# The norm's root in the up and gate stages: spread over the partitions by a store and a broadcast load instead of a matmul with a diagonal

## The chip, the cores and the metric

The kernel runs on one core of a Trainium2 chip. The metric is the device time of one execution in microseconds, the median of several runs. A core has TensorE (PE, matmuls; its weight loads are shown as PEld), VectorE (DVE), ScalarE (ACT), GpSimd (POOL) and SyncE (SP). SP, ACT and POOL also issue the transfers between the core's memory and DRAM, each in the order of its own queue: an issue that has to wait holds up what stands behind it on that engine.

## The reference

One layer of a streaming encoder on 512 tokens with 2048 channels, in float32. Cut to what matters here:

```
h = rms_norm(x, norm_mix_w);  proj = h @ w_in            # attention and gated linear attention, 16 units here
x = x + concat(y_attention, y_linear) @ w_out            # stage "wo"
h = rms_norm(x, norm_ffn_w)
u = causal_depthwise_conv(h @ w_ffn_up)                  # stage "up", 44 units
x = x + (gelu(u_gate) * u_val) @ w_ffn_down              # stages "dn0", "dn1", "dn2"
h = rms_norm(x, norm_ple_w)
g = sigmoid(h @ w_ple_gate)                              # stage "pg", 8 units
x = x + g * (p @ w_ple_proj)
return rms_norm(x, final_norm_w)
```

`rms_norm(x, w)` is `x * rsqrt(mean(x*x) + 1e-6) * w`, with one root per token. The root is a factor of a whole token, so it can be multiplied in after the matmul. This is what the kernel does in "up" and "pg": the channels' weights go into the operand, the matmul runs on the un-normalised values, and its result is multiplied by the root.

## The kernel before

Channels lie on the 128 partitions and tokens along the free dimension: a tile of activations is 128 x 512, and a unit of a stage makes two such tiles. Each stage's matrix product is cut by a Strassen-like scheme into seven products (P1, P2, P6, P5, P7, P3, P4 in `PLAIN`, L33) of blocks and sums of blocks. Each operand is held as a rounded part and a remainder, and a product is made of three passes over its blocks: 24 matmuls of 128x128 by 128x256 with 8 blocks.

**Steps.** The host code writes the order of the work out as a list of steps, one product of one unit each. The first two units of a stage are interleaved product by product (14 steps), and so are the last two. A step `i` does, in this order: the items of an agenda that are due now (`k` 0 and 1), the rounded half of the weight page of step `i + 2` on ScalarE (`prep_high`), its remainder on VectorE (`prep_low`), its own 24 matmuls, then later agenda items, the norm's step, and the read-out of the product from PSUM into the unit's tile `u` (`collect`; the first product of a quarter on ScalarE, the others on VectorE). Weight pages are named `l` (loaded as they are) or `s` (sums of blocks), and the two halves go to one of three places in the tile `w` in turn, so the page of step `i + 2` can be made once product `i - 1` is done. The engines work through their instructions in the order in which they were written; they run ahead of each other as far as the waits on data and buffers allow. The loads of weight pages are issued on SP whenever a page becomes free (`issue`, L430), with POOL adding a second block to some of them. Scratch copies for later stages (`dn_S`, `pg_S`) use the same queues.

**The norm.** In the stages marked `chained` (and `wo` excepted) the sum of squares `acc` (128 x 512) of the stage before is complete only while the first pair of units runs. `norm_step` (L1106) is called after the matmuls of each step with the step's number within the stage:
- at 11, `mean_square` (L1081) makes four matmuls against a column of ones: the mean square of each token, now with tokens on the partitions (128 x 4, in `ms`);
- after the read-out of step 11, `norm_root` (L1121) adds epsilon on VectorE and takes the square root on ScalarE;
- at 12, `rstd_end` (L1095) takes the reciprocal and does one Newton step on VectorE: four small instructions on `tok`. The root then has to come from 128 x 4 to a tile `rb` that has all 512 tokens on each of the 128 partitions. VectorE multiplies the identity by each of the four columns (`dg`, four blocks of 128 x 128, a diagonal each);
- at 13, TensorE multiplies a matrix of ones with `dg` in float32, 128 x 512, into the PSUM bank `pb`, in which each row is now the whole root;
- at 14, ScalarE copies `pb` to `rb`.

**Who reads `rb`.** In "up" each unit's tile is multiplied by `rb` at the start of `after_up` (L680), in "pg" at the start of `after_gate` (L719; the sigmoid follows a step later in ScalarE's order). When a unit's items begin is set by `pace` and `late` (L1618 to L1624): the first unit of "up" not before step 22 of the stage, the first unit of "pg" not before step 15. `late` shifts a unit by some steps more; its key counts the unit from the end of the stage.

Of the kernel before, what the change touches and what calls it, by code (L numbers as in the profile page):

```python
# [8 lines left out]
F32 = mybir.dt.float32  # L9
F32R = mybir.dt.float32r  # L10
I32 = mybir.dt.int32
AF = mybir.ActivationFunctionType
ALU = mybir.AluOpType

P = 128
T = 512
# [4 lines left out]
TT = T // P  # L21
# [21 lines left out]
def encoder_block(ctx: ExitStack, tc: tile.TileContext, A, out):  # L43
    nc = tc.nc
# [3 lines left out]
    tp = ctx.enter_context(tc.tile_pool(name="tmp", bufs=1))  # L48
# [21 lines left out]
    vec, act, ten = InOrder(nc.vector), InOrder(nc.scalar), InOrder(nc.tensor)  # L70
# [8 lines left out]
    ident = cp.tile([P, P], F32, name="ident")  # L79
    make_identity(nc, ident)  # L80
    ones = cp.tile([P, P], F32, name="ones")
# [8 lines left out]
    rb = cp.tile([P, T], F32, name="rb")  # L90
# [19 lines left out]
    late = []  # L110
# [9 lines left out]
    def psum_aux(name):  # L120
        return aux[0](name)
# [171 lines left out]
    def scratch(name, shape):  # L293
        return dp.tile(list(shape), F32, name=name)
# [214 lines left out]
    def prep(i, own=None):  # L509
        prep_low(prep_high(i, own))  # L510

    def prep_high(i, own=None):
        if i >= len(steps):
            return None
        unit, prod = steps[i]
        name = PRODUCTS[prod][0]
        n = unit.stage.kb * P
        make(unit, name)
        if prod == unit.order[0] and unit.sums in ("dve", "s3"):
            make(unit, "S1")  # L520
        if i + 1 < len(steps):
            nxt, p = steps[i + 1]
            q = PRODUCTS[p][0]
            if (nxt is unit or nxt.paired) and (q != "S4" or "P6" in nxt.w) and (unit, q) != (front.units[6], "S2"):
                make(nxt, q)
        if i > 0 and steps[i - 1][1] == "P6" and steps[i - 1][0].paired:
            make(steps[i - 1][0], "S4")
        key = name
        if unit.sums != "memory":
            key = {"S4": "S2"}.get(name, "L21" if name == "S3" and unit.sums != "dma" else name)  # L530
        raw = unit.w[key]
        hi, lo = own or weight_pages(places.get(i, 24))
        act.activation(hi[:, :n], raw[:, :n], AF.Copy)
        unit.w[prod] = hi, lo
        return unit, key, hi[:, :n], lo[:, :n], raw[:, :n]

    def prep_low(p):
        if p:
            unit, key, hi, lo, raw = p
            vec.tensor_tensor(lo, raw, hi.bitcast(F32), ALU.subtract)  # L540
            used(unit, key)
# [7 lines left out]
    def product(unit, prod, at=None, between=None):  # L549
        if prod == "PP":  # L550
            return embedding(unit)
        _, op, b = PRODUCTS[prod]
        fresh = b not in unit.banks
        if fresh:
            unit.banks[b] = bank("acc" + b)
        t = unit.banks[b][1][:, 0:256]
        hi, lo = unit.w[prod]
        st = unit.stage
        kb = st.kb

        for p in range(3):
            for k in range(kb):
                if p * kb + k == at:
                    between()
                x = st.piece(op, k)[:, p % 2]
                w = (hi, hi, lo)[p][:, k * P:k * P + P]
                kw = {} if fresh else {"skip_group_check": True}
                ten.matmul(t, w, x, start=fresh and p == k == 0, stop=p == 2 and k == kb - 1, **kw)
# [33 lines left out]
    def load_x(src, unit):  # L602
        unit.xs = page("c", "xs").rearrange("p (s t) -> p s t", s=2)
        load = nc.sync.dma_start(unit.xs, src[unit.u])
        if unit.stage is wo and unit.pos < 3:
            tc.keep_in_program_order(load)
# [56 lines left out]
    def after_norm(dst, xd, col):  # L663
        def after(unit):
            if unit.last is not None:
                return [(1, 0, lambda: nc.sync.dma_start(dst[unit.u], unit.xs))] + squares(unit, 6 + unit.last * 2)
            return [(0, 1, lambda: residual(dst, unit)), (1, 2, lambda: weighted(col, unit)),
                    (2, 1, lambda: store_pair(xd, unit.u, unit.o[:, 0, :], unit.o[:, 1, :]))] + squares(unit, 3 + (unit.head == 1))
        return after
# [49 lines left out]
    def after_gate(unit):  # L719
# [9 lines left out]
    stages = [Stage("wo", list(range(8)), 8, mixd, blk2(A["w_out"]), after_norm(streams[1], h2d, nffn), "s3", "dma", ends=("memory", None),  # L729
                    begin=lambda u: load_x(streams[0], u), begin_at=10, chained=True)]  # L730
# [176 lines left out]
    for ci, n in enumerate(CHUNKS):  # L907
# [2 lines left out]
                            "dve", "dma", begin=(lambda u: load_x(streams[1], u)) if ci == 2 else None, begin_at=0, late={},  # L910
                            ends=("memory" if ci != 1 else None, "memory" if ci == 2 else None)))
    stages.append(Stage("pg", list(range(8)), 8, h3d, blk2(A["w_ple_gate"]), after_gate, "dma", "dma", last=HALVES, ends=("memory", None),
                        begin=load_gate, begin_at=9, chained=True, pace=(15, 5.3), late={}))
    summed = [u for st in (stages[0], stages[1], stages[2], stages[5], stages[4]) for u in st.units if u.sums == "memory"]
    assert [u.stage.name for u in summed[::2]] == ["wo", "up", "dn0", "pg", "dn2", "dn2"]
    stages[4].quarter = last_quarter(lambda: stages[7], nple)
# [6 lines left out]
    base = {}  # L923
# [26 lines left out]
    for a, b in zip(stages[2:], stages[3:]):  # L950
        i0 = base[a.units[-1]]
        for n, p in enumerate(PLAIN):
            op = PRODUCTS[p][1]
            for g in range(2):
                start = 2 * n + 2 + g
                if g and b.chained:
                    start = max(start, 5)
# [123 lines left out]
    def mean_square(c):  # L1081
        n = (c.stop - c.start) // P
        ms = psum_aux("ms")
        for t in range(n):
            ten.matmul(ms[:, t:t + 1], acc[:, c.start + t * P:c.start + t * P + P], ones[:, 0:1], start=True, stop=True)
        return ms[:, :n]
# [8 lines left out]
    def rstd_end(w):  # L1095
        n = w.shape[1] // 4
        a, y, t, r = (w[:, n * q:n * q + n] for q in range(4))
        vec.reciprocal(y, y)
        vec.tensor_tensor(t, y, y, ALU.mult)
        vec.scalar_tensor_tensor(t, t, -0.5, a, ALU.mult, ALU.mult)  # L1100
        vec.scalar_tensor_tensor(r, t, 1.5, y, ALU.add, ALU.mult)
        return r

    norm = {}

    def norm_step(i):  # L1106

        if i == 11:
            norm["ms"] = mean_square(slice(0, T))
        elif i == 12:  # L1110
            norm["dg"] = tp.tile([P, T], F32, tag="dg", name="dg")
            r = rstd_end(norm["w"])
            for t in range(TT):
                vec.tensor_scalar(norm["dg"][:, t * P:(t + 1) * P], ident, r[:, t:t + 1], None, ALU.mult)
        elif i == 13:
            norm["pb"] = psum_aux("pb")
            ten.matmul(norm["pb"], ones, norm["dg"], start=True, stop=True)
        elif i == 14:
            act.activation(rb, norm["pb"], AF.Copy)

    def norm_root():  # L1121
        norm["w"] = rstd_begin(norm["ms"])
# [456 lines left out]
    for i, (unit, prod) in enumerate(steps[:-4]):  # L1579
        st = unit.stage  # L1580
        now[0] = i
        todo = sorted(agenda[i], key=lambda x: x[0])
        for k, f in todo:
            if k == 0:
                f()

        behind = i == base[front.units[6]]
        if not behind:
            coming = prep_high(i + 2) if i < len(steps) - 5 else None
        for k, f in todo:  # L1590
            if k == 1:
                f()
        if behind:
            coming = prep_high(i + 2)
        prep_low(coming)
        product(unit, prod)
        for k, f in todo:
            if 1 < k < 9:
                f()
        if st.chained and st is not wo:  # L1600
            norm_step(i - base[st.units[0]])
        if i == len(steps) - 5:
            add_gated(units[-2], 1, lo_half)
        if i - len(steps) in EARLY:
            p, op, g = EARLY[i - len(steps)]
            t = xtile(op, g, "last")
            prep(len(steps) + p, (t[:, 0, :], t[:, 1, :]))
        collect(unit, prod)
        for k, f in todo:
            if k == 9:  # L1610
                f()
        if st.chained and st is not wo and unit.head is not None and i == base[unit] + 11:
            norm_root()
        if st is stages[-1] and unit.last is not None:
            if prod == "P4" and unit is units[-2]:
                times_norm(unit, 1, lo_half)
        elif prod == unit.order[-1]:
            begin = i + 1  # L1618
            if st.pace:
                begin = max(begin, base[st.units[0]] + int(st.pace[0] + st.pace[1] * unit.pos))  # L1620
            if unit.pos - len(st.units) in st.late:
                begin += st.late[unit.pos - len(st.units)]
            for at, k, f in st.after(unit):
                agenda[begin + at].append((k, f))  # L1624
# [211 lines left out]
```

## Time and profile before

| | |
|---|---|
| Runs before | 2201.5 us median of 3 (2201.16 to 2205.98) |
| Span of the profiled execution | 6266.3 us; no other time of that execution is recorded |
| TensorE busy, instructions | 6253.6 us, 18248 |
| VectorE busy | 1910.0 us |
| ScalarE busy | 1349.7 us |
| GpSimd busy | 215.6 us |
| Granted TensorE clock | 1.000 |
| Moved by DMA | 561.39 MB, 200037 packets |
| Up stage's `ms` matmuls, spreading matmul | start at 2614.51 and 2631.21 us |
| Gate stage's `ms` matmuls, spreading matmul | start at 5920.51 and 5937.21 us |

The page shows one execution taken by the hardware profiler. Its span is 2.85 times the median of the timed runs, so a place in the trace is not a place in time of a timed run. A row of the order of time reads: start, duration, engine, line, operation, written tile<-read tiles, engine shape (TensorE only), shapes, count, and in brackets the idle time of the engine before it and what ended it. Rows of TensorE stand for several matmuls in a row (x24 is one product). SPq and ACTq are the issues of transfers on these engines; the list of DMA issues gives, at the end of a row, the median time from issue to landing. Nearly all work has line 64, the helper that records instructions, so tiles tell the places apart.

### The profile page before, as it was taken

To read this page: it belongs to the slowest core of one execution; us is meant where nothing else is said; L and a number is where in the kernel's file an instruction comes from. 1 tells how busy PE (TensorE), PEld (TensorE's weight loads), DVE (VectorE), ACT (ScalarE), POOL (GpSimd) and SP (SyncE) were. 2 spreads that over 40 slices of the span, in tenths; PEclk is the share of its full clock that TensorE was granted. 3 is DMA by queue.
4 is the path that set the end of the run, shared out by engine and by line. 5 is a ranking of instruction groups with operands and counts; after the bars stand their busy time and mean duration, and the time that the engine had idled before them with its cause. 6 is when DMAs were issued, how large, how long until landed. Compare 5 with 4: busy or idle time off the path is not lost.

```text
span 6266.3 us, 45637 instructions
## 1 busy us (share of the span) xinstructions
PE 6253.6 (100%) x18248; PEld 5819.7 (93%) x18248; DVE 1910.0 (30%) x2585; ACT 1349.7 (22%) x1960; POOL 215.6 (3%) x261
## 2 busy tenths in 40 slices
PE   9999999999999999999999999999999999999999
PEld 5555999988989799999999999999999999999999
DVE  2222222222222233333333333333333232233333
ACT  2111111222221222222222222222222121222322
POOL 0000000000000000000000000000000000000000
DMA  1123222222222334344444443333333242333432
GB/s 67 34 81 64 61 71 57 72 74 63 70 70 87 110 100 122 101 108 116 113 113 103 112 107 92 83 78 87 79 108 95 61 113 70 109 101 114 121 110 88
DMA packets 200037, 561.39 MB, mean 90 GB/s; under 512 B 21808, under 2 KB 64048, under 8 KB 199824
## 3 DMA queue, kind: packets, MB, share of 16 engines
q1 hardware_dynamic: 163184, 431.28, 21.0%
q0 software_dynamic: 34656, 124.27, 11.5%
q8 instruction: 143, 2.34, 0.2%
q10 hardware_dynamic: 1984, 2.92, 0.1%
q14 instruction: 70, 0.57, 0.0%
HBM read 484.99 MB, written 119.54 MB: 96 GB/s over the span
## 4 chain that ended last, share of the span: by engine, by line
PE 100%; DVE 0%; issue 0%; DVEq 0%; ACT 0%; POOL 0%; POOLq 0%
PE accA L64 48%; PE accC L64 24%; PE accB L64 12%; PE v L64 5%; PE vaA L64 2%; PE vaC L64 1%; PE pp L64 1%; PE psc L64 1%; PE ptr L64 1%; PE py L64 1%; PE po L64 1%; PE vaD L64 1%; PE vaB L64 1%; PE plr L64 0%; PE pu L64 0%; PE pat L64 0%
## 5 line engine op out<-in xcount | busy, mean ns | idle before, releaser
L64 PE MATMUL accA<-h,w 128*128 128x256 f32 x5088 | 1695.5, 563 | 0.0
L64 PEld LDWEIGHTS accA<-h,w 128*128 128x128 f32 x5088 | 1673.7, 473 | 13.1 <-issue 11.6
L64 PE MATMUL accC<-h,w 128*128 128x256 f32 x4248 | 1347.7, 542 | 0.0
L64 PEld LDWEIGHTS accC<-h,w 128*128 128x128 f32 x4248 | 1330.8, 454 | 1.6 <-issue 0.6
L64 DVE TENSOR_TENSOR w<-s,w 128x1024 fp32r<-128x1024 f32 (+1 forms) x381 | 458.4, 1203 | 1100.4 <-ACT w L64 1100.4
L64 DVE TENSOR_TENSOR w<-l,w 128x1024 fp32r<-128x1024 f32 (+1 forms) x320 | 383.2, 1197 | 612.1 <-ACT w L64 607.6
L64 ACT ACTIVATE u<-accA 128x256 f32<-128x256 f32 x302 | 116.1, 384 | 2033.4 <-PE accA L64 2033.4
L64 ACT ACTIVATE w<-l 128x1024 fp32r<-128x1024 f32 (+1 forms) x320 | 331.8, 1037 | 956.1 <-PE accC L64 557.4
L64 ACT ACTIVATE w<-s 128x1024 fp32r<-128x1024 f32 (+1 forms) x381 | 395.0, 1037 | 327.5 <-PE accB L64 203.2
L64 PE MATMUL accA<-up_R,w 128*128 128x256 f32 x1056 | 325.3, 531 | 0.0
L64 PE MATMUL accA<-up_N,w 128*128 128x256 f32 x1056 | 324.2, 530 | 0.0
L64 PE MATMUL accB<-up_R,w 128*128 128x256 f32 x1056 | 323.7, 529 | 0.0
L64 PEld LDWEIGHTS accA<-up_R,w 128*128 128x128 f32 x1056 | 320.5, 441 | 1.6 <-issue 0.8
L64 PEld LDWEIGHTS accA<-up_N,w 128*128 128x128 f32 x1056 | 320.6, 442 | 0.0
L64 PEld LDWEIGHTS accB<-up_R,w 128*128 128x128 f32 x1056 | 320.5, 442 | 0.0
L64 PE MATMUL v<-w,h 128*128 128x512 f32 x384 | 318.6, 1100 | 0.0
L64 PEld LDWEIGHTS v<-w,h 128*128 128x128 f32 x384 | 165.2, 431 | 150.5 <-issue 150.1
L64 DVE TENSOR_TENSOR s<-s,l 128x1024 f32<-128x1024 f32 (+1 forms) x176 | 211.2, 1200 | 0.0
L64 DVE TENSOR_TENSOR u<-u,accC 128x256 f32<-128x256 f32 x102 | 43.0, 421 | 547.7 <-PE accC L64 547.7
L64 DVE TENSOR_TENSOR u<-u,accA 128x256 f32<-128x256 f32 x98 | 41.3, 421 | 510.4 <-PE accA L64 510.4
L64 DVE TENSOR_TENSOR u<-u,accB 128x256 f32<-128x256 f32 x100 | 42.1, 421 | 479.4 <-PE accB L64 479.4
L64 ACT ACTIVATE u<-accC 128x256 f32<-128x256 f32 x98 | 37.7, 384 | 603.5 <-PE accC L64 603.5
(303 smaller groups left out, 5554.9 us busy)
## 6 DMA issues: line engine op xcount, KB each, us to landing
l<-in_w_up SPq DMA_DIRECT2D x132, 512.0 KB, 3.5
s<-in_w_up SPq DMA_DIRECT2D x84, 512.0 KB, 3.5
s<-in_w_up POOLq DMA_DIRECT2D x84, 512.0 KB, 5.5
l<-in_w_dn SPq DMA_DIRECT2D x56, 448.0 KB, 3.4
l<-in_w_blk SPq DMA_DIRECT2D x48, 512.0 KB, 3.5
s<-in_w_blk SPq DMA_DIRECT2D x32, 512.0 KB, 3.5
s<-in_w_blk POOLq DMA_DIRECT2D x32, 512.0 KB, 6.1
l<-in_w_out SPq DMA_DIRECT2D x28, 512.0 KB, 3.6
```

The lines of the kernel that those rows point to most:

```text
L64: ins = f(*args, **kw)
```

## The change

The diagonal, the spreading matmul and the copy out of PSUM are gone. In their place, at step 12, the root (128 x 4, in core memory) is stored to a scratch tensor `rootd` of 4 x 128 words in DRAM, transposed on the way, so that the 512 tokens lie in a row. Later `rb` is loaded from it with the same row read for all 128 partitions. In "up" both transfers are issued on SP, the load at step 14. In "pg" both are issued on ScalarE's queue, the load at step 13, and the first unit's items after its products begin one step later than before (`late={-8: 1}`: the eighth unit from the end is the first).

```diff
     stages.append(Stage("pg", list(range(8)), 8, h3d, blk2(A["w_ple_gate"]), after_gate, "dma", "dma", last=HALVES, ends=("memory", None),
-                        begin=load_gate, begin_at=9, chained=True, pace=(15, 5.3), late={}))
+                        begin=load_gate, begin_at=9, chained=True, pace=(15, 5.3), late={-8: 1}))
...
     norm = {}
+    rootd = scratch("rootd", (TT, P))
 
-    def norm_step(i):
+    def norm_step(i, load, queue):
 
         if i == 11:
             norm["ms"] = mean_square(slice(0, T))
         elif i == 12:
-            norm["dg"] = tp.tile([P, T], F32, tag="dg", name="dg")
-            r = rstd_end(norm["w"])
-            for t in range(TT):
-                vec.tensor_scalar(norm["dg"][:, t * P:(t + 1) * P], ident, r[:, t:t + 1], None, ALU.mult)
-        elif i == 13:
-            norm["pb"] = psum_aux("pb")
-            ten.matmul(norm["pb"], ones, norm["dg"], start=True, stop=True)
-        elif i == 14:
-            act.activation(rb, norm["pb"], AF.Copy)
+            queue.dma_start(rootd.rearrange("t p -> p t"), rstd_end(norm["w"]))
+        elif i == load:
+            queue.dma_start(rb, rootd.rearrange("t p -> (t p)")[None, :].broadcast_to([P, T]))
...
         if st.chained and st is not wo:
-            norm_step(i - base[st.units[0]])
+            norm_step(i - base[st.units[0]], *((13, nc.scalar) if st is stages[-1] else (14, nc.sync)))
```

How this moves the instructions on the queues that wait or are waited for is shown in the prediction, where it is used: on ScalarE in the first pair of "pg", and on SP in the first pair of "up". On TensorE nothing moves but for the row `pb<-dg,ones`, which is gone in both stages:

```order
L64 MATMUL accA<-h_102,w 128x256 x7
L64 MATMUL pb<-dg,ones 128x512
L64 MATMUL accA<-pg_R_23315,w 128x256
```

This is the order before, at the end of step 13 of "pg"; in the change the first matmul of step 14 follows the last one of step 13.

## The prediction

> **What bounds the kernel now.** I read the page first (engines, then the chain that ended last), then the order of time around the two stretches the change touches.
>
> ```profile
> span 6266.3 us, 45637 instructions
> PE 6253.6 (100%) x18248; PEld 5819.7 (93%) x18248; DVE 1910.0 (30%) x2585; ACT 1349.7 (22%) x1960; POOL 215.6 (3%) x261
> PE 100%; DVE 0%; issue 0%; DVEq 0%; ACT 0%; POOL 0%; POOLq 0%
> ```
>
> TensorE bounds the profiled execution from end to end. But that execution spans 6266.3 us and the timed median is 2201.5 us, 0.351 of it, and nothing in the page explains the difference. So a sum made in the trace does not carry over as it stands. Two readings are possible. In the *even* reading every duration shrinks by 0.351. In the *PE-only* reading the profiled execution merely ran TensorE's instructions slowly, and VectorE, ScalarE and DMA keep their durations. The second passes the test it could fail: VectorE's 1910.0 us fit into 2201.5 us (87%). It is the stricter one for this change, because waits that 7 us products hide in the trace may show under shorter ones. I work with PE-only and keep the even reading as a bound.
>
> The unit of time is one product of 24 matmuls, one step of the agenda. Two neighbours of the gate stage start 7.17 us apart:
>
> ```profile
> 5968.14 7.34 PE L64 MATMUL accA<-h,w 128*128 128x256 f32 x24
> 5975.31 7.34 PE L64 MATMUL accC<-h,w 128*128 128x256 f32 x24
> ```
>
> 7.17 x 0.351 = 2.52 us is my estimate for a timed product.
>
> **What the matmul with the diagonal costs.** The up stage first: the two last products of the first pair (one row of 48 matmuls), the spreading matmul, and the next unit's products.
>
> ```profile
> 2616.77 14.60 PE L64 MATMUL accA<-h,w 128*128 128x256 f32 x48
> 2620.27 0.88 DVE L64 TENSOR_SCALAR dg<-ident,tok 128x128 f32<-128x128 f32 x4
> 2631.21 2.64 PE L64 MATMUL pb<-dg,ones 128*128 128x512 f32 x2
> 2632.48 8.55 PE L64 MATMUL accA<-up_R,w 128*128 128x256 f32 x24
> 2633.56 7.01 PEld L64 LDWEIGHTS accA<-up_R,w 128*128 128x128 f32 x23 [0.83 <-issue]
> 2633.89 0.60 ACT L64 ACTIVATE rb<-pb 128x512 f32<-128x512 f32 x1 [1.15 <-PE pb L64]
> 2640.74 7.34 PE L64 MATMUL accB<-up_R,w 128*128 128x256 f32 x24
> ```
>
> From 2616.77 to 2640.74 are 23.97 us for three products of 7.17 (21.51) and pb: pb makes 2.46 us of difference. 1.27 of it is pb's own place (2631.21 to 2632.48), the rest is the next product starting slowly behind it (the 0.83 us before its second weight load). The gate stage is the same:
>
> ```profile
> 5922.64 14.74 PE L64 MATMUL accA<-h,w 128*128 128x256 f32 x48
> 5923.12 1.04 ACT L64 ACTIVATE w<-l 128x1024 fp32r<-128x1024 f32 x1
> 5924.20 1.23 DVE L64 TENSOR_TENSOR w<-l,w 128x1024 fp32r<-128x1024 f32 x1 [1.22 <-ACT w L64]
> 5925.74 0.36 DVE L64 SCALAR_TENSOR_TENSOR tok<-tok 128x4 f32<-128x4 f32 x2
> 5926.14 0.87 DVE L64 TENSOR_SCALAR dg<-ident,tok 128x128 f32<-128x128 f32 x4
> 5930.37 0.39 ACT L64 ACTIVATE u<-accA 128x256 f32<-128x256 f32 x1 [6.20 <-PE accA L64]
> 5930.65 1.05 ACT L64 ACTIVATE w<-l 128x1024 fp32r<-128x1024 f32 x1
> 5937.21 2.64 PE L64 MATMUL pb<-dg,ones 128*128 128x512 f32 x2
> 5937.41 0.38 ACT L64 ACTIVATE u<-accA 128x256 f32<-128x256 f32 x1 [5.71 <-PE accA L64]
> 5938.48 8.42 PE L64 MATMUL accA<-pg_R,w 128*128 128x256 f32 x24
> 5938.77 1.23 DVE L64 TENSOR_TENSOR w<-s,w 128x1024 fp32r<-128x1024 f32 x1 [5.82 <-ACT w L64]
> 5940.52 1.23 DVE L64 TENSOR_TENSOR u<-u,rb 128x1024 f32<-128x1024 f32 x1 [0.53 <-ACT rb L64]
> 5946.74 7.34 PE L64 MATMUL accB<-pg_R,w 128*128 128x256 f32 x24
> ```
>
> 24.10 - 21.51 = 2.59 us. Both together: 5.05 us at most; by the even reading 5.05 x 0.351 = 1.77 us at least, as long as TensorE is the bound there. I take pb's own place unshrunk and let the slow start behind it go, 2 x 1.27 = **2.5 us gained**: a pass over 512 columns is real work, while the gap before a weight load belongs to the slow issue of this execution.
>
> The four diagonal tiles on VectorE (0.88 and 0.87 us) and the copy to rb on ScalarE (0.60 us, twice) go too. I cost them at nothing: ScalarE sits idle for 5.71 and 6.20 us and VectorE for 5.82 us before the next product's work in these rows, and in the PE-only reading VectorE still has 13% free. Were VectorE the bound in both stretches, its 1.75 us would be the gain instead, less than the 2.5.
>
> **What the store and the load cost.** No transfer of 4-byte pieces occurs before, so the store (512 of them, 128 partitions x 4) is bounded by other rows.
>
> ```profile
> q1 hardware_dynamic: 163184, 431.28, 21.0%
> g_N<-tp SPq DMA_DIRECT2D x44, 128.0 KB, 1.8
> bias<-in_bias SPq DMA_DIRECT2D x16, 256.0 KB, 2.5
> wo_S<-in_w_out SPq DMA_DIRECT2D x8, 512.0 KB, 4.6
> dn_S<-dn_S POOLq DMA_DIRECT2D x8, 448.0 KB, 8.2
> ```
>
> Below: 1.8 us, the fastest landing. Above: q1's packets average 0.21 x 16 x 6266.3 / 163184 = 0.129 us; 512 over 16 engines are 32 x 0.129 = 4.1 us, on top of 1.8 makes 5.9. The slowest row, 8.2 us, is the far end. I take 4 us. The load writes 256 KB, as bias does: 2.5 us (1.8 to 4.6).
>
> The Trainium skill, DMA: Bandwidth & Descriptors, section Rules for kernel authors, speaks against such a store: a strided last dimension becomes one descriptor per element. In its section Anatomy of one DMA a transfer (of GpSimd's kind) has a fixed part of about 2.0 us, and its section Bandwidth has 10.5 ns for a small packet: as an estimate from this page the store would take 2.0 + 32 x 0.0105 = 2.3 us, nothing would wait for it, and the sum would be 2199.0. No trace so far has such a store.
>
> Gate stage, ScalarE's order, before and in the change (l and s are weight pages whose rounded half goes to w, accA is read out of PSUM into u):
>
> ```order
> L64 ACTIVATE tok<-tok 128x4
> L64 ACTIVATE w<-l_23819 128x1024
> L64 ACTIVATE u<-accA 128x256
> L64 ACTIVATE w<-l_23851 128x1024
> L64 ACTIVATE u<-accA 128x256
> L64 ACTIVATE w<-s_24176 128x1024
> L64 ACTIVATE rb<-pb 128x512
> ```
>
> ```order
> L64 ACTIVATE tok<-tok 128x4
> L64 ACTIVATE w<-l_23814 128x1024
> L1112 DMA rootd<-tok 128x4x1
> L64 ACTIVATE u<-accA 128x256
> L64 ACTIVATE w<-l_23846 128x1024
> L1114 DMA rb<-rootd 128x512
> L64 ACTIVATE u<-accA 128x256
> L64 ACTIVATE w<-s_24167 128x1024
> ```
>
> Two waits have come into ScalarE's queue: for VectorE's root ahead of step 13's read-out and weight page, and for the store's landing ahead of step 14's page, which step 16's product needs. Count from the start of step 12 (5922.64), with timed products of 2.52 us:
> - The root is done at 5926.10 - 5922.64 = 3.5. Nothing in that chain waits for a later product, so it does not shrink. ScalarE issues the store, reads out accA (0.39) and makes the page of step 15 (1.05): done at about 5.4, needed at 3 x 2.52 = 7.6. Hidden by 2.2 us.
> - The store lands at 3.5 + 0.4 + 4 = 7.9 (5.7 to 12.1). Load issue 0.4, read-out 0.38, page 1.05: step 16's page is ready at 9.7 (7.5 to 13.9) and needed at 4 x 2.52 = 10.1. At my value it is hidden by 0.4 us; at the far end TensorE stands still for 3.8 us. The next page, step 17's, follows one read-out and page later: 11.2 against 12.6.
> - rb arrives at 8.3 + 2.5 = 10.8. VectorE's first use was moved one step, behind the low halves of steps 16 and 17 and the read-out of step 15 (which ends at 10.1) and a sum of 1.2 us, so not before 11.7. Hidden.
>
> I book 0.5 us of loss here for a store somewhat slower than 4 us. If the cover were gone, the cost would be the 3.8 us above.
>
> Up stage, SP's order in the change:
>
> ```order
> L64 DMA s_9067<-in_w_up 128x1024
> L1112 DMA rootd<-tok 128x4x1
> L458 DMA dn_S_9164<-in_w_dn 128x1024
> L64 DMA s_9198<-in_w_up 128x1024
> L1114 DMA rb<-rootd 128x512
> L64 DMA l_9228<-in_w_up 128x1024
> L64 DMA l_9232<-in_w_up 128x1024
> ```
>
> Before, the same weight and dn_S loads stand there without the two L111x rows. What queues behind the load's wait are the l pages of the unit after next.
>
> ```profile
> 2622.34 0.33 SPq L64 DMA_DIRECT2D s<-in_w_up  x1
> 2641.07 0.38 ACT L64 ACTIVATE u<-accA 128x256 f32<-128x256 f32 x1 [6.58 <-PE accA L64]
> 2642.43 1.23 DVE L64 TENSOR_TENSOR w<-s,w 128x1024 fp32r<-128x1024 f32 x1 [8.43 <-ACT w L64]
> 2643.69 7.48 SPq L64 DMA_DIRECT2D l<-in_w_up  x3
> ```
>
> The s page went out only after the root anyway (2622.34 against 2620.27). The three l pages go out behind VectorE's half of the page that ScalarE makes after reading out step 14, in my count at 3 x 2.52 + 0.4 + 1.05 + 1.2 = 10.2; SP is free again between 5.7 and 12.1, so they are up to 2 us late, with more than one unit (7 x 2.52 = 17.6 us) before they are read. Nothing. rb is first read at step 22 in this stage, some 20 us after the root. Nothing. POOL's queue is not touched: 244 rows before and after.
>
> **The sum.** -2.5 + 0.5 = -2.0 us. Against the profiled execution's span, where 7.17 us products hide every wait, it would be 6266.3 - 5.05 = 6261.3; on the timed median 2201.5 - 2.0 = **2199.5 us**.
>
> **Rivals.**
> - *ScalarE's wait decides* (slower). At the far end the store lands at 12.1, and step 16 starts 3.8 us late: -2.5 + 3.8 = +1.3, so 2202.8. It decides once the store needs more than 4.4 us; past about 10.5 us, with the read-outs and pages queued up behind it, the loss passes 6.5 us and the result 2205.9. For it: 512 pieces are something this kernel never sent. Against: 8.2 us is a row of accumulating transfers of 448 KB.
> - *The matmul was not on the path* (no change). If in the timed run TensorE waits for VectorE or ScalarE in the paired products anyway, taking pb out moves the wait: 2201.5. For it: VectorE at 87% on average, and these steps also split the operands. Against: the idle time before VectorE's rows is 5 us of 7.17 here.
> - *The whole stall goes* (faster). If the slow start behind pb is real time too, 5.05 us go and nothing comes: 2196.5. For it: the 0.83 us gap stands behind both pb's. Against: it would have to be the one thing that does not shrink in a run 2.85 times as fast.
> - *Even reading*: 1.77 us go, every wait is hidden as in the trace: 2199.7, the forecast within noise.
>
> **How the numbers follow.** Forecast with the even reading 0.52; not on the path 0.20; whole stall 0.16; ScalarE's wait 0.12. About 0.2% (4.4 us) is what a measurement of this kernel can tell from no change; the three runs before span 4.8 us. Faster than 2197.1: the whole stall and some spread of the forecast, 0.20. Slower than 2205.9: the tail of ScalarE's wait and the spread of the runs, 0.09. The rest, 0.71, is no change. The range takes the whole stall below and ScalarE's wait with the before runs' spread above: 2196.0 to 2205.5.
>
> **What would show it.** Right: no pb row in either stretch, the products around both places 7.17 us apart throughout, the profiled span some 5 us shorter; the store landing within 6 us of its issue; no idle time of VectorE before the first u<-u,rb named after DMA. Wrong: idle time of ScalarE ending with the store, longer than 4.4 us; a weight page landing after its first reader is ready; or a time outside 2196.0 to 2205.5, which means that the shape of the timed run differs from both readings.

## The result and the profile after

The changed kernel takes 2211.86 us (median of 5 runs, 2210.13 to 2214.03), the kernel before 2201.5 us (5 runs, 2199.93 to 2205.98). The ratio is 1.0039, with an interval of 1.0028 to 1.0051: slower by 6 to 11 us, where 2 us of gain were forecast, and outside the range of 2196.0 to 2205.5. Single executions of 3127.87 us (the kernel before, granted clock 0.653) and 5677.53 us (an experiment, 1.000) also occurred and stand in no ratio here; the profiled execution of 6266.3 us on which the prediction rests resembles the second.

So the profile of the changed kernel, which runs at the timed speed, needs a partner that does the same. The kernel before was profiled again (experiment e_before below). Its page, engines of it:

```profile
span 2204.8 us, 45637 instructions
PE 2182.9 (99%) x18248; PEld 2132.2 (97%) x18248; DVE 1874.5 (85%) x2585; ACT 1321.6 (60%) x1960; POOL 215.1 (10%) x261
```

And the page of the changed kernel, span and engines:

```profile
span 2208.4 us, 45624 instructions
PE 2179.6 (99%) x18244; PEld 2130.6 (96%) x18244; DVE 1873.2 (85%) x2577; ACT 1319.7 (60%) x1958; POOL 214.9 (10%) x261
```

The busy times fell, as instructions are gone: TensorE by 3.3 us, VectorE by 1.3, ScalarE by 1.9. The span did not. By busy times alone the change would be a gain; the loss is time in which TensorE, though 99% busy on average, does nothing or works slowly in one place. That place is the gate stage. From the start of its `ms` matmuls to the end of the span, the kernel before takes 2204.8 - 2062.24 = 142.6 us and the changed one 2208.4 - 2056.45 = 151.9 us, 9.4 us more (in the text below: "the tail"; one execution each, and two kernels that are equal from there on differ by 0.7). Its first steps before, in the order of time:

```profile
2062.24 1.02 PE L64 MATMUL ms<-ones,acc 128*128 128x1 f32 x8
2063.13 5.69 PE L64 MATMUL accA<-h,w 128*128 128x256 f32 x48
2069.20 1.13 PE L64 MATMUL pb<-dg,ones 128*128 128x512 f32 x2 [0.38 <-DVE dg L64]
2069.76 3.30 PE L64 MATMUL accA<-pg_R,w 128*128 128x256 f32 x24
...
2072.90 2.89 PE L64 MATMUL accB<-pg_R,w 128*128 128x256 f32 x24
```

The same steps in the changed kernel; ACTq rows are ScalarE's issues of transfers:

```profile
2056.45 1.05 PE L64 MATMUL ms<-ones,acc 128*128 128x1 f32 x8
2057.36 5.90 PE L64 MATMUL accA<-h,w 128*128 128x256 f32 x48
2062.16 0.36 DVE L64 SCALAR_TENSOR_TENSOR tok<-tok 128x4 f32<-128x4 f32 x2
2062.56 0.38 ACTq L1112 DMA_DIRECT2D rootd<-tok  x1
2063.10 2.99 PE L64 MATMUL accA<-pg_R,w 128*128 128x256 f32 x24
2065.92 2.99 PE L64 MATMUL accB<-pg_R,w 128*128 128x256 f32 x24
2074.30 0.33 ACTq L1114 DMA_DIRECT2D rb<-rootd  x1
2074.67 0.38 ACT L64 ACTIVATE u<-accA 128x256 f32<-128x256 f32 x1 [10.36 <-DMA rootd<-tok]
2074.95 1.05 ACT L64 ACTIVATE w<-s 128x1024 fp32r<-128x1024 f32 x1
2075.90 0.38 ACT L64 ACTIVATE u<-accA 128x256 f32<-128x256 f32 x1
2076.33 5.34 PE L64 MATMUL accA<-pg_N,w 128*128 128x256 f32 x24 [7.42 <-ACT u L64]
2080.78 1.23 DVE L64 TENSOR_TENSOR u<-u,rb 128x1024 f32<-128x1024 f32 x1 [0.83 <-DMA rb<-rootd]
2081.51 2.90 PE L64 MATMUL accC<-h,w 128*128 128x256 f32 x24
```

The reader is to see three things. ScalarE issues the store at 2062.56 and the load at 2074.30; after one read-out and one page it is idle for 10.36 us, for the store. Behind the load stand the read-out of step 13, the weight page of step 16 and the read-out of step 14, so TensorE waits 7.42 us before step 16's product (`pg_N`). What the trace names as the end of that wait is the last of the three, done at 2076.28; the rounded half of the page was done at 2076.00. And that product takes 5.2 us (2076.33 to 2081.51) where its neighbours take 2.7 to 2.8. In the chain that ended last the store's landing stands with 11.72 us, between VectorE's last instruction on `tok` and ScalarE's issue of the load. The stretches of this place, with TensorE's granted clock (columns: stretch, its length, then busy time and instructions of PE, PEld, DVE, ACT and POOL, granted clock, busy share of the DMA engines, GB/s):

```profile
2057.00:2068.00 11.00, 11.00 (x95) 11.00 (x95) 6.56 (x12) 3.37 (x5) 0.00 (x0) 1.00 1.04 382
2068.00:2076.30 8.30, 0.91 (x8) 0.71 (x6) 0.27 (x1) 1.63 (x4) 1.74 (x2) 0.69 0.73 49
2076.30:2081.40 5.10, 5.07 (x24) 5.08 (x25) 4.27 (x5) 3.15 (x3) 0.00 (x0) 0.50 1.06 206
2081.40:2090.00 8.60, 8.60 (x77) 8.60 (x77) 8.12 (x9) 6.87 (x10) 0.00 (x0) 1.00 0.82 302
```

The slow product ran at a granted clock of 0.50. It took some 2.4 us more than its neighbours, a second cost of the same wait. The landings of the two transfers in the changed kernel (from the lists of DMA issues of the gate stage and of the up stage, in this order; the last number is us from issue to landing):

```profile
rb<-rootd ACTq DMA_DIRECT2D x1, 256.0 KB, 6.5
rootd<-tok ACTq DMA_DIRECT2D x1, 2.0 KB, 11.7
...
rb<-rootd SPq DMA_DIRECT2D x1, 256.0 KB, 9.2
rootd<-tok SPq DMA_DIRECT2D x1, 2.0 KB, 10.5
```

### The profile page after: what moved, and what is told of

Same layout as the page of the kernel before. It is cut to its first block, busy times and chain, and to the rows that moved or that the text cites. A ratio compares the mean times of both kernels' runs of the same rounds, so it can differ in the third digit from the quotient of the medians.

```text
span 2208.4 us, 45624 instructions
## 1 busy us (share of the span) xinstructions
PE 2179.6 (99%) x18244; PEld 2130.6 (96%) x18244; DVE 1873.2 (85%) x2577; ACT 1319.7 (60%) x1958; POOL 214.9 (10%) x261
## 4 chain that ended last, share of the span: by engine, by line
PE 83%; DVE 7%; DMA 6%; ACT 2%; issue 2%; SPq 0%; POOL 0%; ACTq 0%; DVEq 0%; POOLq 0%
PE accA L64 42%; PE accC L64 21%; PE accB L64 11%; PE v L64 4%; DVE w L64 2%; PE pp L64 1%; DMA s<-in_w_blk 1%; ACT w L64 1%; PE py L64 1%; DVE h L64 1%; PE psc L64 1%; DMA x3d<-xs 1%; PE vaA L64 1%; DVE s L64 1%; DMA wva_P_r<-in_w_v_a 1%
## 5 line engine op out<-in xcount | busy, mean ns | idle before, releaser
L64 PE MATMUL accA<-h,w 128*128 128x256 f32 x5088 | 613.4, 278 | 1.7 <-ACT u L64 1.3
L64 PEld LDWEIGHTS accA<-h,w 128*128 128x128 f32 x5088 | 594.6, 188 | 4.7 <-ACT u L64 2.2
L64 PE MATMUL accC<-h,w 128*128 128x256 f32 x4248 | 509.4, 277 | 0.0
L64 PEld LDWEIGHTS accC<-h,w 128*128 128x128 f32 x4248 | 494.3, 188 | 0.3
L64 ACT ACTIVATE w<-s 128x1024 fp32r<-128x1024 f32 (+1 forms) x381 | 394.8, 1037 | 32.9 <-DVE s L64 15.5
L64 DVE TENSOR_TENSOR s<-s,l 128x1024 f32<-128x1024 f32 (+1 forms) x176 | 211.4, 1201 | 14.7 <-DMA s<-in_w_blk 11.7
L64 PE MATMUL accA<-up_R,w 128*128 128x256 f32 x1056 | 126.6, 277 | 0.0
L64 PE MATMUL accA<-up_N,w 128*128 128x256 f32 x1056 | 126.6, 277 | 0.0
L64 PEld LDWEIGHTS accB<-up_R,w 128*128 128x128 f32 x1056 | 123.0, 188 | 0.0
L64 PEld LDWEIGHTS accA<-up_R,w 128*128 128x128 f32 x1056 | 122.9, 188 | 0.0
L64 PEld LDWEIGHTS accA<-up_N,w 128*128 128x128 f32 x1056 | 122.9, 188 | 0.0
L64 PE MATMUL v<-w,h 128*128 128x512 f32 x384 | 88.7, 392 | 0.2 <-ACT h L171 0.2
L64 PEld LDWEIGHTS v<-w,h 128*128 128x128 f32 x384 | 71.9, 188 | 15.9 <-issue 0.5
```

The costliest lines, as they stand in the source:

```text
L64: ins = f(*args, **kw)
```

## The experiments

Two theories were set against each other. One: the store's landing is late, and ScalarE, which waits for it in its queue, brings the whole loss. The other: VectorE's wait for `rb` at the first unit's reader would bring it too, whichever engine issues. Beside them stood the question of whether the size of the gain, 2.5 us, and the free up stage were right. All ratios are to the kernel before, run on the same chip.

### The kernel before, profiled again

No edit.

> The kernel before, unchanged, to have a second profile of it: the first spans 6266.3 us, the profile of the changed kernel 2208.4 us. Every theory: ratio 1.000 within 0.1%, about 2201.5 us. If the first profile was an execution with slow TensorE instructions, the span is about 2200 us now, products of the gate stage are 2.72 us apart as in the changed kernel, and pb takes about 1 us in each of the two places; if it were usual for this kernel, the span is near 6266 us again.

Measured: 2204.56 us, ratio 0.9995 (0.9986 to 1.0004), and the span of 2204.8 us shown above. Its list of DMA issues holds the rows from which the prediction took its prices:

```profile
DMA packets 200037, 561.39 MB, mean 255 GB/s; under 512 B 21808, under 2 KB 64048, under 8 KB 199824
...
g_N<-tp SPq DMA_DIRECT2D x44, 128.0 KB, 6.3
...
bias<-in_bias SPq DMA_DIRECT2D x16, 256.0 KB, 4.5
```

`g_N` lands after 6.3 us and not 1.8, `bias` after 4.5 and not 2.5. The same bytes pass in 0.35 of the time; that the transfers then stand in each other's way is the likely reason, but no run changes the load alone. VectorE's busy time, 1874.5 us against 1910.0, did keep its size.

### One stage alone

The up stage alone by store and load, the gate stage as before:

```diff
-            norm_step(i - base[st.units[0]], *((13, nc.scalar) if st is stages[-1] else (14, nc.sync)))
+            norm_step(i - base[st.units[0]], *((0, None) if st is stages[-1] else (14, nc.sync)))   # None: dg, pb and copy as before
-                        ... chained=True, pace=(15, 5.3), late={-8: 1}))
+                        ... chained=True, pace=(15, 5.3), late={}))
```

> Store and load in the up stage alone; the gate stage keeps the matmul with the diagonal and late={}. Theory A (ScalarE's queue in the gate stage stands on the store's landing, and that is the whole loss): 0 to 2 us below before, 2200.5 us, since SP's wait costs nothing and one pb is gone. Rival C (both stages lose, by the store's traffic and SP's blocked queue): 3 to 6 us above before.

The gate stage alone, `(14, nc.sync)` replaced by `(0, None)` instead and `late={-8: 1}` kept:

> Store and load in the gate stage alone, as in the change; the up stage keeps the matmul. Theory A: the whole loss and a little more, 10 to 12 us above before, 2212 us, with ScalarE idle for about 10 us until the store lands. Rival C: about half of the loss, 4 to 7 us above before.

Measured: up alone 2204.04 us, ratio 0.9999 (0.9990 to 1.0009); gate alone 2212.87 us, ratio 1.0034 (1.0021 to 1.0047), its tail 2207.4 - 2056.39 = 151.0 us, 8.5 more than before. The gate stage alone lost somewhat less than the 10 to 12 us expected, but the up stage alone lost nothing, so the loss is the gate stage's. In the up stage the store is nearly as slow (10.5 us in the changed kernel) and TensorE stands still for none of it: nothing that it needs soon waits behind it. The first reader in the up stage and what stands around it, in the changed kernel's order of time:

```profile
799.30 0.38 SPq L1112 DMA_DIRECT2D rootd<-tok  x1
...
809.86 0.33 SPq L1114 DMA_DIRECT2D rb<-rootd  x1
819.50 1.22 DVE L64 TENSOR_TENSOR u<-u,rb 128x1024 f32<-128x1024 f32 x1
```

`rb` lands at 809.86 + 9.2 = 819.1, and the reader at 819.50 has no idle time before it. So the 20 us between root and reader, on which the prediction rested, are used up but for 0.4 us: the cover held narrowly.

### The two waits apart

First both transfers of the gate stage on SP, so that ScalarE waits for neither of them:

```diff
-            norm_step(i - base[st.units[0]], *((13, nc.scalar) if st is stages[-1] else (14, nc.sync)))
+            norm_step(i - base[st.units[0]], *((14, nc.sync) if st is stages[-1] else (14, nc.sync)))
```

> The change, but the gate stage's store and load are issued on SP with the load at step 14, as in the up stage; the first reader stays at step 16. Theory A (ScalarE's wait alone): within 2 us of before, 2200 us, ScalarE has no idle time that ends with the store. Rival B (the root reaches rb too late for its first reader whoever issues it; VectorE then stands in ScalarE's place): rb lands some 19 us after the root, VectorE waits about 10 us at the first u<-u,rb, TensorE for 6 to 8, and the time is 6 to 9 us above before.

Measured: 2213.1 us, ratio 1.0037 (1.0024 to 1.0050), tail +9.4. No gain over the change. Its order of time:

```profile
2062.90 0.37 SPq L1112 DMA_DIRECT2D rootd<-tok  x1
2071.49 2.88 PE L64 MATMUL accC<-h,w 128*128 128x256 f32 x24
2074.30 0.32 SPq L1114 DMA_DIRECT2D rb<-rootd  x1
2079.55 1.23 DVE L64 TENSOR_TENSOR u<-u,rb 128x1024 f32<-128x1024 f32 x1 [9.10 <-DMA rb<-rootd]
2080.81 1.06 ACT L64 ACTIVATE u<-u 128x1024 f32<-128x1024 f32 x1 [10.46 <-DVE u L64]
2081.77 0.37 ACT L64 ACTIVATE u<-accA 128x256 f32<-128x256 f32 x1
2082.19 5.49 PE L64 MATMUL accA<-h,w 128*128 128x256 f32 x24 [7.81 <-ACT u L64]
```

ScalarE does not wait for the store, step 16 runs on time, and step 17 too (2071.49). But VectorE stands 9.10 us before the first reader, with the remainder of step 18's page behind it, and ScalarE then stands 10.46 us before the first unit's sigmoid (`u<-u`), which needs what VectorE multiplied. Behind the sigmoid stands the read-out of `accA`, done at 2082.14, and that is what the trace names as the end of TensorE's 7.81 us before step 18. So the wait comes to TensorE by ScalarE's queue again, now over VectorE's reader. This is rival B of the expectation (6 to 9 us expected, about 8 measured): the late `rb` costs as much as the late store, and in the change the two waits overlap.

Then the readers are moved too, the first unit's items by five more steps and the second's by two, once with the transfers on SP and once on ScalarE as in the change. A control has the moved readers alone, on the kernel before.

```diff
-                        ... pace=(15, 5.3), late={-8: 1}))
+                        ... pace=(15, 5.3), late={-8: 6, -7: 2}))      # e_gate_sp_late: with (14, nc.sync); e_act_late: as in the change
```

> Both of the gate stage's transfers on SP (load at step 14) and the first reader of rb moved to step 21, the second to 22 (late={-8: 6, -7: 2}), after rb has landed (in the run with SP alone at about step 20). Theory AB (two waits, ScalarE's for the store and VectorE's for rb, each enough for the whole loss, and nothing else): 0 to 3 us below before, no idle time of ScalarE or VectorE behind either transfer. Rival D (the store's traffic slows the weight pages, or the moved reader delays the units behind it): still 3 us or more above before.

> The change with its transfers left on ScalarE (load at step 13) and the readers at steps 21 and 22. Theory AB: ScalarE's wait of about 10 us is still there, TensorE stands still for about 7 us, 7 to 10 us above before. Rival B alone (only the reader's place counts): within 2 us of before.

> The kernel before with the matmul, and the gate stage's first readers moved to steps 21 and 22 (late={-8: 6, -7: 2}) as in the two late kernels; no store, no load of the root. Theory D (the moved reader delays the units behind it): 4 to 7 us above before, with TensorE standing for 2 to 3 us some 20 to 30 us later. If it is within 2 us of before, the loss of the late kernel with SP came from the store's traffic.

| | us | ratio (95%) | tail against before |
|---|---|---|---|
| control: readers later, matmul kept | 2208.31 | 1.0015 (1.0004 to 1.0025) | +5.5 |
| readers later, transfers on SP | 2209.84 | 1.0029 (1.0018 to 1.0041) | +6.5 |
| readers later, transfers on ScalarE | 2215.16 | 1.0057 (1.0044 to 1.0070) | +15.5 |

With both waits out of the way, the kernel with store and load has a tail of 149.04 us, 0.9 more than the control's 148.11, about what two tails differ by. With ScalarE's wait left in, it has 9.9 more. So each of the two waits is enough for about the whole loss. That nothing is left without them is not shown: the expectation of 0 to 3 us below before was missed (5.6 above). The control explains the larger part of that, but it still carries the matmul, which costs 1.2 us in this stage, and the timed medians lie 2.8 us apart, with overlapping intervals. Some 2 us by the tails may be due to the store's traffic or to chance. Of the other two expectations, the kernel with ScalarE's wait lost a little more than the 7 to 10 us (10.9), and the control less than the 4 to 7 us (2.8, its tail 5.5). What TensorE waited for in the tail, in the views of waits (us in total, times, longest): readers later and transfers on ScalarE,

```profile
PE accA L64 <- ACT u L64: 8.7, 2, 7.5
PE accC L64 <- ACT u L64: 2.5, 1, 2.5
```

with transfers on SP,

```profile
PE accC L64 <- ACT u L64: 2.7, 1, 2.7
PE accA L64 <- ACT u L64: 1.7, 1, 1.7
```

and in the control:

```profile
PE accC L64 <- ACT u L64: 2.7, 1, 2.7
```

The 2.7 us stand in the control as well: they come with the moved readers. The product behind them is slow again (4.45 us in the control, 2102.23 to 2106.68). Moving the readers out of the way is therefore no way out. It takes away the wait for `rb` and brings another, for a read-out on ScalarE, likely because the moved items now come all at once.

### A store of 16-byte pieces

Instead of 512 pieces of 4 bytes the store writes 128 of 16 bytes (each partition's four tokens in a row). The load then brings the tokens in another order, and ScalarE's copy puts it right; the transfers are on SP, and the first unit's items come four steps later.

```diff
-            queue.dma_start(rootd.rearrange("t p -> p t"), rstd_end(norm["w"]))
+            queue.dma_start(rootd.rearrange("t p -> (t p)").rearrange("(p t) -> p t", t=TT), rstd_end(norm["w"]))
         elif i == load:
-            queue.dma_start(rb, rootd.rearrange("t p -> (t p)")[None, :].broadcast_to([P, T]))
+            norm["sp"] = tp.tile([P, T], F32, tag="dg", name="rbp")
+            queue.dma_start(norm["sp"], rootd.rearrange("t p -> (t p)")[None, :].broadcast_to([P, T]))
+        elif i == load + 4:
+            act.activation(rb.rearrange("q (t p) -> q t p", t=TT), norm["sp"].rearrange("q (p t) -> q t p", t=TT), AF.Copy)
```

> In both stages the store writes each partition's four roots as one piece: 128 pieces of 16 bytes in place of 512 of 4. The row in DRAM is then ordered by partition, so the load (SP, step 14) goes to a spare page and ScalarE turns it into rb at step 18 (0.6 us); first reader in the gate stage at step 19. Theory P (the store's time is its number of pieces): it lands in 3 to 5 us in place of 10.5 to 11.7, rb's page is there by step 17, and the time is within 2 us of before. Rival Q (the store queues behind the loads, or a store that small always takes this long): it lands after 9 to 12 us, ScalarE waits at step 18 for some 5 us, and the time is 2 to 6 us above before.

Measured: 2207.24 us, ratio 1.0013 (1.0003 to 1.0022), tail +4.8. The store's landings in the lists of DMA issues, up stage and then gate stage:

```profile
rootd<-tok SPq DMA_DIRECT2D x1, 2.0 KB, 1.4
...
rootd<-tok SPq DMA_DIRECT2D x1, 2.0 KB, 6.8
```

The same 2 KB land after 1.4 us instead of 9.4 to 10.6 in the up stage, and after 6.8 instead of 11.1 to 11.7 in the gate stage (one profile against five in each stage). The landings fit neither theory as stated (3 to 5 us or 9 to 12), and the time, 2.9 us above before (0.7 to 4.8), reaches into both. What is left of the loss has again another place. It is a wait of TensorE well behind the root:

```profile
2082.21 1.22 DVE L64 TENSOR_TENSOR u<-u,rb 128x1024 f32<-128x1024 f32 x1
2101.59 5.49 PE L64 MATMUL accA<-h,w 128*128 128x256 f32 x24 [3.43 <-ACT u L64]
```

The reader of `rb` itself waits for nothing, so the wait for `rb` is not what is left. The 3.43 us, the 2.6 us by which the product behind them is slow (2101.59 to 2106.88), less the 1.2 us of the matmul, make 4.8 us, the whole of this tail. The wait resembles the control's, where items moved by six steps brought 2.7 us; a control with four steps was not run. The kernel does not beat the one before.

### What a small store costs under the weight stream

Two kernels add stores of constant values, which nothing reads, to the kernel before, on SP through the up stage and at the end of the gate stage, in four shapes: 512 pieces of 4 bytes into one row as in the change ("adj"), 512 of 4 bytes spread 256 bytes apart ("far"), 128 of 16 bytes ("piece", in the first of the two kernels "p16"), 128 of 4 bytes ("one").

```diff
+        if i % 7 == 3 and 35 <= i < 300:
+            small_store(i)       # the four shapes in turn, 128x4 or 128x1 of ident; second kernel: issued where it is written
```

> The kernel before (matmul with the diagonal in both stages) with 38 more stores on SP in the up stage, one in every seventh step from 38 on, that nobody reads, of constant data, in four shapes in turn: adj, 512 pieces of 4 bytes that lie next to each other in DRAM, as in the change; far, 512 pieces of 4 bytes 256 bytes apart; p16, 128 pieces of 16 bytes next to each other; one, 128 pieces of 4 bytes next to each other. The time itself is not of interest, the landings are. Theory P (number of pieces): adj and far about equal at 9 to 12 us, p16 and one about equal at 1.5 to 5 us. Rival N (pieces that share a stretch of DRAM hinder each other): far clearly below adj, and one above p16 or like adj per piece. Rival Q (waiting behind other transfers): all four alike.

> As the run with four shapes of store before it, but each store is kept in its place in SP's order (in that run they all went out within the first 150 us, on top of one another): one every seventh step of the up stage, in turn adj (512 pieces of 4 bytes, next to each other), far (512 of 4 bytes, 256 bytes apart), piece (128 of 16 bytes), one (128 of 4 bytes). Nobody reads them. Theory P (number of pieces): adj and far alike at 9 to 12 us, piece and one alike at 1.5 to 5 us. Rival N (pieces that share a stretch of DRAM hinder each other): far clearly below adj. Rival Q (waiting behind other transfers): all four alike.

Measured: in the first, the stores were issued early in the program, on top of each other, and landed after medians of 11.0, 11.7, 11.1 and 10.9 us. That says nothing about shapes. In the second they stood where they should:

```profile
far<-ident SPq DMA_DIRECT2D x11, 2.0 KB, 11.7
piece<-ident SPq DMA_DIRECT2D x11, 2.0 KB, 10.8
one<-ident SPq DMA_DIRECT2D x9, 0.5 KB, 12.5
adj<-ident SPq DMA_DIRECT2D x9, 2.0 KB
```

Under the stage's weight loads a small store of any shape seen took a median of 10.8 to 12.5 us, even one of 0.5 KB; this is the rival of waiting behind other transfers. The profile gives no landing for the change's own shape ("adj"). Read with e_16b: in the up stage, where the DMA engines moved 9 GB/s (the change) and 32 GB/s (16-byte pieces) in the last 1.3 or 1.4 us before the store was issued, the pieces decided. Under the weight stream every shape was late by its median, and the 6.8 us of the 16-byte store in the gate stage lie within what single stores of that shape took here (4.5 to 13.6 us). Whether it is the number of pieces or the neighbouring words in DRAM that makes the change's store slow on nearly empty engines was not separated. The kernels themselves took 2274.15 us (before 2205.47) and 2255.53 us (before 2200.63), single runs: 40 small stores cost 55 us and more.

### Nothing instead of the matmul

The gate and up stages keep the root in `tok` and spread it in no way; the multiplications by `rb` then use old contents, so these two norms' roots are left out of the result.

```diff
         elif i == 12:
-            queue.dma_start(rootd.rearrange("t p -> p t"), rstd_end(norm["w"]))
-        elif i == load:
-            queue.dma_start(rb, rootd.rearrange("t p -> (t p)")[None, :].broadcast_to([P, T]))
+            rstd_end(norm["w"])                                   # and late={}
```

> The root is computed in the up and gate stages but not spread: no diagonal, no matmul, no copy, no store and no load; rb keeps the root of the first norm, so this kernel leaves out the two later norms' roots. First reader at step 15 as before. It is what any way to spread the root that costs nothing could give. From the second profile of the kernel before, pb and the slow product behind it make 1.3 us in the up stage and 1.6 us in the gate stage: the prediction's term of 2.5 us would show as 2 to 3 us below before (ratio 0.9987). If the matmul was hidden, no difference.

Measured: 2200.26 us against 2203.5, ratio 0.9986 (0.9978 to 0.9995): 3.1 us less, 1.1 to 4.8 by the interval. With the readers where they were, this bounds what any other way of spreading these two roots could gain.

## Why the prediction was wrong

**TensorE bounds the kernel, and removing `pb` gains 2.5 us: right.** Taking the spreading out altogether gained 3.1 us (1.1 to 4.8). In the second profile of before, the three products and `pb` of the gate stage take 2072.90 - 2063.13 = 9.77 us, against 2065.92 - 2057.36 = 8.56 us after: 1.2 us in that stage. The choice to count `pb`'s own place unshrunk was right by its sum and not by its parts: `pb` holds 0.56 us (2069.20 to 2069.76), a wait for `dg` 0.38, and the product behind it 0.3 to 0.4 more than others. The rival of the whole stall (5.05 us) lies outside that interval.

**"VectorE, ScalarE and DMA keep their durations" (the PE-only reading): wrong for DMA, and the reason for the store's price below.** The engines kept theirs to about 2%. The landings did not: they had been read in an execution whose transfers ran at 561.39 MB / 6266.3 us = 90 GB/s, and in a timed one they share 255 GB/s. `g_N`, taken as the lower bound of a store, went from 1.8 to 6.3 us. The test that was made for the reading, that VectorE's busy time fits into the median, says something about engines and nothing about transfers.

**"I take 4 us" for the store: wrong, and this is the step that failed.** It landed after 11.7 us, past the far end of 8.2 us. All bounds came from the long execution. Worked out again with the rows of the second profile, by the same steps, they are 6.3 us below, 6.3 + 32 x 0.118 = 10.1 us above (an estimate; a packet of q1 took 0.118 us on average, hardly less than the 0.129 before) and 11.3 us for the slowest row it named, `dn_S<-dn_S`. All of these lie past the 4.4 us at which ScalarE's wait decides by the prediction's own count. At the upper two that count gives losses of 3.2 and 4.4 us instead of a gain. How much of the 11.7 us is owed to the 512 pieces and how much to the weight stream stays open: in the up stage it was the pieces, under the stream no shape was reliably fast.

The estimate worked out from the Trainium skill, DMA: Bandwidth & Descriptors, was 2.3 us. It divides the page's 10.5 ns for a packet by the 16 engines, though the page, in its section Bandwidth, has that figure from 0.67 us for the 64 packets of a whole transfer; undivided, the estimate is 2.0 + 512 x 0.0105 = 7.4 us. The measured 10.5 and 11.7 decide against both. The rule in its section Rules for kernel authors, that a strided last dimension becomes one descriptor per element and is better made contiguous, agrees with 1.4 us for the 16-byte store in the up stage.

**The root is done 3.5 us after step 12's start: 1.7 us short.** It was done at 2062.52 - 2057.36 = 5.2 us. The chain from the square root on is as long as forecast; it starts 2.1 us after step 12's start (2059.43) and not 0.4 (5923.01 in the long execution). There VectorE had stood idle for 1.55 us before the root's first instruction; in the timed one it comes to it straight from the read-outs and remainders of earlier steps.

**"Hidden by 0.4 us" (step 16's page behind ScalarE's wait): wrong in the size, right in the place.** This was the rival *ScalarE's wait decides*, with a chance of 0.12. Put the measured numbers in its count, from step 12's start: root 5.2, store landed at 2074.30 - 2057.36 = 16.9, then load issue, read-out and page in 1.8: 18.7. Step 16 would have started at 2068.75 (2065.92 and one product of 2.83; the prediction had 2.52), that is 11.4. The difference is 7.3 us; the trace has 7.42. The prediction's own sign of being wrong, idle time of ScalarE of more than 4.4 us that ends with the store, came with 10.36 us. It had named 10.5 us of landing as the point past which the loss passes 6.5 us and the result 2205.9; its count gives 6.1 us of standstill there and 2201.5 + 6.1 - 2.5 = 2205.1. It gave that point too small a chance.

**"rb hidden": wrong.** The reader was ready when the prediction said (not before 11.7 us; in e_gate_sp 2079.55 - 9.10 - 2057.71 = 12.7), but `rb` came at 21.8 us there and not at 10.8. This wait alone costs as much as ScalarE's, which no rival had.

**What no step had: the half clock behind a standstill.** Step 16's product took 5.2 us at a granted clock of 0.50 after the idle 7.42 us, and step 18's in e_gate_sp was as slow after 7.81 (5.49 in its row, where others have 2.88 to 2.99). This adds 2.4 us to the first of these waits and 2.6 to the second. The Trainium skill, TensorE: Matmul & The Clock Gate, section "Part 1: The HAM clock gate (the "warmup" mystery)", gives half rate after an idle window of about 3.4 us and full rate after about as long a busy one. The stretches above agree with half rate after 7.42 us. They differ in the other two: 0.50 lasted for 5.1 us of work, and in the kernel with later readers and the transfers on ScalarE a standstill of 2.48 us was enough (0.50 over the 2.3 us behind it). The measurement decides.

**The sum by measured terms.** In the gate stage: `pb` -1.2, standstill +7.4, half clock +2.4, together +8.6, against +9.4 in the two tails. The up stage's three products and `pb` took 9.42 us before (798.96 to 808.38 in its order of time) and 8.56 after (794.11 to 802.67): another -0.9. The sum of +7.7 lies inside the 6 to 11 us of the timed ratio.

**Up stage at nothing: right.** It gave a ratio of 0.9999 (0.9990 to 1.0009), and the gain of its own `pb` is too small to show there. **The even reading** fell with VectorE's busy time, which did not shrink, and with the landings, and **the matmul not on the path** with e_no_spread.

## What to carry to other kernels

Before a trace is used for prices, compare its span with the timed runs. Here it was 2.85 times as long, its transfers ran at 90 GB/s instead of 255, and their landings were too short to price by. A small store to DRAM followed by a load of the same words is a latency of two landings (here 11.7 + 6.5 us under a weight stream), so count every instruction queued behind the load's issue and every reader behind the load, and ask of each what TensorE has left to do by then. A wait that leaves TensorE idle for several microseconds costs more than its length: here 2.4 us on top of 7.4.

## What the runs showed of the hardware that was not expected

- TensorE's granted clock is 0.50 for the first 5.1 us after a standstill of 7.42 us. A standstill of 3.43 us was enough in the 16-byte experiment, and those of 2.48 to 2.75 us in the three kernels with later readers are followed by products of 4.1 to 4.5 us. From the 16-byte experiment (the standstill and the product behind it, columns as in the stretches above):

```profile
2098.20:2101.60 3.40, 0.01 (x1) 0.01 (x1) 2.31 (x3) 3.40 (x7) 0.00 (x0) 0.91 1.03 405
2101.60:2106.80 5.20, 5.20 (x24) 5.20 (x25) 3.50 (x3) 4.60 (x6) 0.00 (x0) 0.50 0.96 332
```

- A 2 KB store of 512 pieces holds up large transfers issued beside it. In the up stage two `dn_S` loads of 512 KB landed after a median of 15.9 us, in the kernel before after 6.8, and one with the 16-byte store after 6.7, each by the list of DMA issues of its own up stage. The stretch of the changed kernel around the store's issue (same columns as above):

```profile
798.00:812.00 14.00, 14.00 (x122) 14.00 (x121) 9.81 (x13) 6.45 (x10) 0.86 (x1) 1.00 0.55 23
```

and of the kernel before, at the same place of the program:

```profile
798.90:812.00 13.10, 13.10 (x107) 12.62 (x107) 9.54 (x19) 6.85 (x11) 1.75 (x2) 1.00 0.70 220
```

The DMA engines are shown 0.55 busy with 23 GB/s, against 0.70 with 220. The kernel with the 16-byte store, which starts from nearly empty DMA engines as the change does, moves 221 GB/s from 798 to 812 us, which points to the 512 pieces as what holds the others up.

- An execution that is 2.85 times as long shows a granted clock of 1.000: the clock does not tell it apart.
